# A hybrid streaming layer: the input turned by VectorE in 32x32 blocks, its K tiles made of strided features

## The chip, the core and the metric

One core of one Trainium2 chip runs the whole program. The metric is the device time of one execution in microseconds (us). TensorE (PE) multiplies, with a separate stream of weight loads (PEld); VectorE (DVE), ScalarE (ACT) and GpSimd (POOL) work element by element; SyncE (SP) only starts transfers here. Each engine has its own list of instructions and takes them in the order of that list; engines wait for one another, and for transfers, by semaphores. On-chip data lies in 128 partitions, in SBUF, and TensorE's results in PSUM.

## The reference, cut to what matters

One layer over 256 prompt tokens and 32 sample tokens, 288 columns in all. The change touches the front of it: the input norm and the projection `w_in`.

```
xn   = rmsnorm(x, norm_mix_pre)                 # x: 288 tokens x 2048 features
proj = xn @ w_in                                # 2048 x 5664: [u 1024 | z 2048 | xBC 2560 | dt 32]
pool = pooling mixer on u
ssd  = Mamba-2 scan on xBC and dt, gated by z
x    = x + rmsnorm(concat[pool, ssd] @ w_out, norm_mix_post)
x    = x + rmsnorm(ConvFFN(rmsnorm(x, norm_ffn_pre)), norm_ffn_post)
```

The outputs are the two token blocks and the new states. Everything is float32.

## The kernel before, in words

**Layout.** Activations lie turned: features on partitions, the 288 tokens along the free axis. A product adds one K tile (128 features) into a 128 x 288 accumulator in PSUM. To keep float32 accuracy with a faster product type, every operand is split into a rounded part and a rest: `split_from` (L113) and `split_w` (L134) let ACT write the rounded part (`xn` L120, `whi` L146) and DVE the rest (L121, `wlo` L147), and `mm3` (L162) multiplies three times (L163, L164, L165). The 32 columns of dt are too narrow for that: `split_narrow` (L151) puts both parts side by side in `both` (ACT L158, DVE L159), and two products per K tile do the work (L185, L186).

**The start.** `input_tiles` (L292) loads a slice of x with the tokens on partitions (L294 for the prompt, L295 for the sample), and turns each K tile with three products against the identity (L299, L300, L301) into PSUM. ACT and DVE split it from there, DVE also copies the turned tile to `xT` (L304), and ACT's queue stores `xT` to DRAM in `xT_d` (L306), for the residual much later. The norm's factor per token is not applied here: it multiplies the results of the projection instead.

**The first projection.** `project` (L167) walks over the 16 K tiles in five steps of 2, 2, 4, 4 and 4, with three weight loads in each step: 256 columns of B, 256 of C, 32 of dt (`O_B`, `O_C`, `O_DT`, L338; the load is L131 in `fetch_w`). That is 16 x (4 x 3 + 2) = 224 products into five accumulators (`first`). The squares of x for the norm are summed by ACT (L348, L349), and TensorE spreads the factor `rs` over all partitions with six passes (`prs`, L355). `parameters` (L309) turns the small weights that came as rows, with nine products against the identity (L281, L325).

**What follows** is a long series of projections of 256 columns each: xs (8), z (8) and u (4) from `w_in`, then `w_out`, `w_up` and `w_down`. Weight tiles (`raw`, `whi`, `wlo`) have four buffers each, accumulators five banks, and three more banks (`aux`) serve the rest.

**The order.** The tile framework's scheduler orders each engine's list by priorities. `tc.high_priority` moves an instruction ahead, and `tc.keep_in_program_order`, called `pin` where it has a name, holds instructions of an engine in the order of the program. In the kernel before, the scheduler is free to mix the first projection with the next one, and does so: the last 44 products of the first projection stand after `prs` and among 25 of the first xs projection.

Of the kernel before, what the change touches and what calls it, by code (L numbers as in the profile page):

```python
# [8 lines left out]
F32 = mybir.dt.float32  # L9
F32R = mybir.dt.float32r  # L10
# [6 lines left out]
P = 128  # L17
# [22 lines left out]
XS_RATE = (0, 0, 1, 0, 1, 0, 1, 0)  # L40
Z_RATE = (1, 0, 1, 1, 0, 1, 1, 0)
TAIL = NT - P


@with_exitstack
def body(
# [77 lines left out]
            )  # L124

    ahead = [0]

    def fetch_w(view, kb, nk, c0, nc_):
        raw = wpool.tile([P, nk, nc_], F32, tag="raw", name="raw")
        with tc.high_priority(offset=ahead[0]):  # L130
            sp.dma_start(out=raw, in_=view[:, kb : kb + nk, c0 : c0 + nc_])  # L131
        return raw

    def split_w(raw, kb, nk, nc_, after=()):  # L134

        out = []
        step = min(nk, 1024 // nc_)
        for k in range(0, nk, step):
            n = min(step, nk - k)
            hi = wpool.tile([P, n, nc_], F32R, tag="hi", name="whi")  # L140
            lo = wpool.tile([P, n, nc_], F32R, tag="lo", name="wlo")
            with ExitStack() as order:
                order.enter_context(tc.high_priority(offset=ahead[0]))
                for ins in after:
                    order.enter_context(tc.issue_after(ins.ins))
                act.activation(hi, raw[:, k : k + n, :], AF.Copy)  # L146
                dve.tensor_tensor(lo, raw[:, k : k + n, :], hi.bitcast(F32), op=ALU.subtract)  # L147
            out.append([(kb + k + i, hi[:, i, :], lo[:, i, :]) for i in range(n)])
        return out

    def split_narrow(raw, kb, nk, nc_, after):  # L151

        both = xin.tile([P, nk, 2, nc_], F32R, tag="both", bufs=2, name="both")
        with ExitStack() as order:
            order.enter_context(tc.high_priority(offset=ahead[0]))
            for ins in after:
                order.enter_context(tc.issue_after(ins.ins))
            act.activation(both[:, :, 0, :], raw, AF.Copy)  # L158
            dve.tensor_tensor(both[:, :, 1, :], raw, both[:, :, 0, :].bitcast(F32), op=ALU.subtract)  # L159
        return [(kb + k, both[:, k, :, :].rearrange("p r c -> p (r c)")) for k in range(nk)]  # L160

    def mm3(out, wh, wl, a, start, stop):  # L162
        pe.matmul(out, wh, a[:, 0, :], start=start, stop=False)  # L163
        pe.matmul(out, wh, a[:, 1, :], start=False, stop=False)  # L164
        pe.matmul(out, wl, a[:, 0, :], start=False, stop=stop)  # L165

    def project(view, groups, acts, ksplit, before=None, done=None, spare=(), hold=(), behind=None):  # L167

# [6 lines left out]
        for i, (kb, n) in enumerate(ksplit):  # L175
            raws = [fetch_w(view, kb, n, c0, w) for c0, w in groups]
            nxt = None
            if before and i + 1 < len(ksplit):
                nxt = before(*ksplit[i + 1])
            m0 = 0  # L180
            for raw, (c0, w) in zip(raws, groups):
                if w < P:
                    for k, both in split_narrow(raw, kb, n, w, after or ()):
                        o = accs[m0][: 2 * w, :]
                        pe.matmul(o, both, acts[k][:, 0, :], start=k == k_first, stop=False)  # L185
                        pe.matmul(o, both, acts[k][:, 1, :], start=False, stop=k == k_last)  # L186
                    continue
# [12 lines left out]
            after = nxt  # L200
# [10 lines left out]
    K16 = [(0, 8), (8, 8)]  # L211


    ident = const.tile([P, P], F32, name="ident")
    make_identity(nc, ident)
    ones = const.tile([P, P], F32, name="ones")
    pool.memset(ones, 1.0)
    tri = const.tile([P, P], F32, name="tri")
    pool.affine_select(
        out=tri, in_=ones, pattern=[[1, P]], compare_op=ALU.is_ge, fill=0.0, base=0, channel_multiplier=-1  # L220
# [24 lines left out]
        pool.memset(e, 0.0)  # L245
        ebuf.append(e)

    start = ExitStack()
    xin = start.enter_context(tc.tile_pool(name="xin", bufs=1))

    g0_in = xin.tile([KD, P], F32, name="g0_in")
    act.dma_start(out=g0_in, in_=rows(norm_mix_pre))
# [5 lines left out]
    xt = xin.tile([P, 2, D_MODEL], F32, name="xt")  # L258
    xs_ = xin.tile([NS, D_MODEL], F32, name="xs_")
    xpv = x_prompt.rearrange("o (b p) d -> p (o b) d", p=P)  # L260
# [17 lines left out]
    def columns(src, n, name):  # L278
        o = const.tile([P, n], F32, name=name)
        p_ = aux([P, n], "pt")  # L280
        pe.transpose(p_, src, ident[:n, :n])  # L281
        dve.tensor_copy(o, p_)
        return o

    g_mix_pre = columns(g0_in, KD, "g0")


    xn = []
    xT = xin.tile([P, KD, NT], F32, name="xT")
    xT_d = dram.tile([P, KD, NT], F32, name="xT_d")  # L290

    def input_tiles(kb, n):  # L292
        c = slice(kb * P, (kb + n) * P)
        sp.dma_start(out=xt[:, :, c], in_=xpv[:, :, c])  # L294
        sp.dma_start(out=xs_[:, c], in_=x_sample[0][:, c])  # L295
        for t in range(kb, kb + n):
            p_ = aux([P, NT], "pt")
            c = slice(t * P, (t + 1) * P)
            pe.transpose(p_[:, 0:P], xt[:, 0, c], ident)  # L299
            pe.transpose(p_[:, P:NP_], xt[:, 1, c], ident)  # L300
            pe.transpose(p_[:, NP_:NT], xs_[:, c], ident[:NS, :NS])  # L301
            a = atile("xn")
            last = split_from(a, p_, g_mix_pre[:, t : t + 1])
            dve.tensor_copy(xT[:, t, :], p_)  # L304
            xn.append(a)
        act.dma_start(out=xT_d[:, kb : kb + n, :], in_=xT[:, kb : kb + n, :])  # L306
        return last

    def parameters():  # L309
        pb = columns(pb_in, 108, "pb")  # L310
# [11 lines left out]
        for i in range(0, 6, 3):  # L322
            p_ = aux([P, 3, NF * 2], "ptf")
            for j in range(3):
                pe.transpose(p_[:, j, :], pf_in[:, i + j, :], ident[: NF * 2, : NF * 2])  # L325
            dve.tensor_copy(pf[:, i : i + 3, :], p_)
        return pb, pah, g_mix_post, g_ffn_pre, g_ffn_post, pa, p_scale, g_ssd, pc, pf

    prm = []

    def first_in(kb, n):
        if kb == 12:
            prm.extend(parameters())
        return input_tiles(kb, n)

    win = w_in.rearrange("o (k p) c -> p (o k) c", p=P)
    O_Z, O_X = D_POOL, D_POOL + D_SSD
    O_B, O_C, O_DT = O_X + D_SSD, O_X + D_SSD + 256, O_X + CONV  # L338
    first = project(
        win, [(O_B, 256), (O_C, 256), (O_DT, HEADS)], xn, [(0, 2), (2, 2), (4, 4), (8, 4), (12, 4)], first_in  # L340
    )

    ahead[0] = 200
    ssum = xin.tile([P, 3], F32, name="ssum")
    pool.memset(ssum, 1.0)
    junk = xin.tile([P, D_MODEL], F32, name="junk")
    for b in range(2):
        act.activation(junk, xt[:, b, :], AF.Square, accum_out=ssum[:, b : b + 1])  # L348
    act.activation(junk[:NS, :], xs_, AF.Square, accum_out=ssum[:NS, 2:3])  # L349
    rs = xin.tile([P, 3], F32, name="rs")  # L350
    act.activation(rs, ssum, AF.Sqrt, bias=eps_t, scale=1.0 / D_MODEL)
    dve.reciprocal(rs, rs)
    p_ = aux([P, NT], "prs")
    for b, (o, n) in enumerate(BLK):
        pe.matmul(  # L355
            p_[:, o : o + n], rs[:n, b : b + 1].broadcast_to([n, P]), ident[:n, :n], start=True, stop=True
        )
    rstd = const.tile([P, NT], F32, tag="spread", bufs=3, name="rstd")
    dve.tensor_copy(rstd, p_)

    pb, pah, g_mix_post, g_ffn_pre, g_ffn_post, pa, p_scale, g_ssd, pc, pf = prm
    start.close()
# [509 lines left out]
    for grp in ((0, 1), (2,), (3,), (4,), (5,), (6,), (7,)):  # L872
# [7 lines left out]
        elif grp[0] == 6:  # L880
            late_in[:] = [state_in(t, t >= LATE + 4) for t in range(LATE, NX)]
        if grp[0] == 0:
            sp.dma_start(out=xT, in_=xT_d)
# [148 lines left out]

    p_f = aux([P, 4], "psum_f")
    fd = dram.tile([NT, D_MODEL], F32, name="fd")
    pin = tc.keep_in_program_order

    def to_tokens(t):

# [182 lines left out]
```

## Time and profile before

| | us |
|---|---|
| median of 3 runs (1354.6 to 1355.04) | 1354.8 |
| the profiled execution | 1354.13 |
| its span, from first to last instruction | 1352.2 |
| PE busy in the span | 1340.3 |
| DVE busy | 883.2 |
| ACT busy | 668.8 |
| POOL busy | 237.7 |

A matmul's recorded duration includes the time in which it drains, beside the next one; what a product costs in a dense row is the distance from start to start, 0.13 us for 288 columns. The same holds, more weakly, for DVE and ACT: the next instruction starts some 0.1 us before the recorded end of the one before, unless it waits for it. In the timeline a line gives start, duration, engine, line, operation, output and inputs; in brackets is how long the engine had been idle, and what released it.

### The profile page before, as it was taken

To read this page: it belongs to the slowest core of one execution; us is meant where nothing else is said; L and a number is where in the kernel's file an instruction comes from. 1 tells how busy PE (TensorE), PEld (TensorE's weight loads), DVE (VectorE), ACT (ScalarE), POOL (GpSimd) and SP (SyncE) were. 2 spreads that over 40 slices of the span, in tenths; PEclk is the share of its full clock that TensorE was granted. 3 is DMA by queue.
4 is the path that set the end of the run, shared out by engine and by line. 5 is a ranking of instruction groups with operands and counts; after the bars stand their busy time and mean duration, and the time that the engine had idled before them with its cause. 6 is when DMAs were issued, how large, how long until landed. Compare 5 with 4: busy or idle time off the path is not lost.

```text
span 1352.2 us, 25779 instructions
## 1 busy us (share of the span) xinstructions
PE 1340.3 (99%) x10217; PEld 1328.7 (98%) x10217; DVE 883.2 (65%) x1519; ACT 668.8 (49%) x1004; POOL 237.7 (18%) x394
## 2 busy tenths in 40 slices
PE   8999999999999999999999999999999999999997
PEld 7999999999999999999999999999999999999997
DVE  6898989679644469977666643335666666664444
ACT  5657767446434455644444433334444444454443
POOL 3132112222214310212121100001111111100110
PEclk9999999999999999999999999999999999999999
DMA  8869995465756536866545545554554554576662
GB/s 264 255 192 283 255 263 162 147 219 154 241 181 210 170 111 196 238 174 196 187 156 166 170 145 167 172 179 156 180 164 156 178 166 156 172 231 184 192 182 89
DMA packets 300136, 252.13 MB, mean 186 GB/s; under 512 B 75729, under 2 KB 293051, under 8 KB 299887
## 3 DMA queue, kind: packets, MB, share of 16 engines
q1 hardware_dynamic: 296942, 243.46, 59.4%
q0 software_dynamic: 2320, 4.65, 1.2%
q10 hardware_dynamic: 752, 2.37, 0.5%
q8 instruction: 80, 1.31, 0.4%
q14 instruction: 42, 0.34, 0.1%
HBM read 236.13 MB, written 14.31 MB: 185 GB/s over the span
## 4 chain that ended last, share of the span: by engine, by line
PE 99%; DMA 0%; DVE 0%; ACT 0%; issue 0%; DVEq 0%
PE acc L163 31%; PE acc L165 31%; PE acc L164 31%; PE pst L852 1%; PE py L562 1%; PE acc L1127 1%; PE acc_x L164 0%; PE acc_x L165 0%; PE acc_x L163 0%; PE py L564 0%; DMA xt<-in_x_prompt 0%; PE pt L299 0%; PE pt L301 0%; PE acc L1128 0%; PE acc L186 0%; PE pt L300 0%
## 5 line engine op out<-in xcount | busy, mean ns | idle before, releaser
L147 DVE TENSOR_TENSOR wlo<-raw,whi 128x1024 fp32r<-128x1024 f32 (+1 forms) x416 | 493.2, 1187 | 346.6 <-ACT whi L146 345.5
L146 ACT ACTIVATE whi<-raw 128x1024 fp32r<-128x1024 f32 (+1 forms) x416 | 426.6, 1027 | 483.1 <-PE acc L164 411.0
L163 PE MATMUL acc<-hn,whi 128*128 128x288 f32 x1376 | 404.6, 295 | 0.0
L164 PE MATMUL acc<-hn,whi 128*128 128x288 f32 x1376 | 403.5, 294 | 0.0
L165 PE MATMUL acc<-hn,wlo 128*128 128x288 f32 x1376 | 403.2, 294 | 0.0
L164 PEld LDWEIGHTS acc<-hn,whi 128*128 128x128 f32 x1376 | 259.8, 189 | 0.1
L165 PEld LDWEIGHTS acc<-hn,wlo 128*128 128x128 f32 x1376 | 259.6, 189 | 0.0
L163 PEld LDWEIGHTS acc<-hn,whi 128*128 128x128 f32 x1376 | 257.3, 187 | 0.1
L163 PE MATMUL acc<-xn,whi 128*128 128x288 f32 x704 | 209.3, 299 | 0.0
L164 PE MATMUL acc<-xn,whi 128*128 128x288 f32 x704 | 207.9, 296 | 0.0
L165 PE MATMUL acc<-xn,wlo 128*128 128x288 f32 x704 | 207.0, 296 | 0.0
L163 PE MATMUL acc<-fa,whi 128*128 128x288 f32 x682 | 201.9, 296 | 0.0
L164 PE MATMUL acc<-fa,whi 128*128 128x288 f32 x682 | 201.9, 296 | 0.0
L165 PE MATMUL acc<-fa,wlo 128*128 128x288 f32 x682 | 201.5, 295 | 0.0
L164 PEld LDWEIGHTS acc<-xn,whi 128*128 128x128 f32 x704 | 133.6, 190 | 0.3
L165 PEld LDWEIGHTS acc<-xn,wlo 128*128 128x128 f32 x704 | 132.8, 189 | 0.3
L163 PEld LDWEIGHTS acc<-xn,whi 128*128 128x128 f32 x704 | 132.4, 189 | 0.5
L164 PEld LDWEIGHTS acc<-fa,whi 128*128 128x128 f32 x682 | 128.6, 188 | 0.0
L163 PEld LDWEIGHTS acc<-fa,whi 128*128 128x128 f32 x682 | 128.1, 188 | 0.0
L165 PEld LDWEIGHTS acc<-fa,wlo 128*128 128x128 f32 x682 | 127.9, 188 | 0.0
L944 POOL COPY fc_stage<-ebuf 128x4 f32<-128x4 f32 x88 | 27.2, 309 | 496.6 <-DVE ebuf L943 454.5
L939 POOL COPY ebuf<-pf 128x2 f32<-128x2 f32 x88 | 74.4, 846 | 126.2 <-DVE fc L950 52.4
(337 smaller groups left out, 1680.6 us busy)
## 6 DMA issues: line engine op xcount, KB each, us to landing
raw<-in_w_up SPq DMA_DIRECT2D x80, 1024.0 KB, 5.2
raw<-in_w_in SPq DMA_DIRECT2D x40, 1024.0 KB, 5.8
raw<-in_w_down SPq DMA_DIRECT2D x32, 1024.0 KB, 5.4
raw<-in_w_out SPq DMA_DIRECT2D x24, 1024.0 KB, 6.2
raw<-in_w_down SPq DMA_DIRECT2D x16, 768.0 KB, 4.8
raw<-in_w_up SPq DMA_DIRECT2D x14, 512.0 KB, 4.3
gb<-g_d SPq DMA_DIRECT2D x8, 832.0 KB, 5.7
raw<-in_w_in SPq DMA_DIRECT2D x6, 512.0 KB, 7.1
```

The lines of the kernel that those rows point to most:

```text
L146: act.activation(hi, raw[:, k : k + n, :], AF.Copy)
L147: dve.tensor_tensor(lo, raw[:, k : k + n, :], hi.bitcast(F32), op=ALU.subtract)
L163: pe.matmul(out, wh, a[:, 0, :], start=start, stop=False)
L164: pe.matmul(out, wh, a[:, 1, :], start=False, stop=False)
L165: pe.matmul(out, wl, a[:, 0, :], start=False, stop=stop)
L562: ins = pe.matmul(y[c, 0:256], xw[:, 0, f_], m[:, h, 0:256], start=True, stop=False)
L852: ins = pe.matmul(st[:, o, :], x_, btok[:, gi, b, :], start=b != 1, stop=b != 0)
L939: pool.tensor_copy(e[:, 258:260], pf[:, 4:6, i])
L944: pool.tensor_copy(fc_stage[:, :, :, i], e[:, 256:324].rearrange("p (s c) -> p s c", c=34)[:, :, 0:2])
L1127: pin(pe.matmul(o, hi, f2[k][:, :, c], start=k == 0, stop=end, skip_group_check=True))
```

## The change

- x is loaded as 32-token blocks: partition 32i + t of `xt` holds token t of each of the nine blocks of 32 (eight of the prompt, one of the sample), for features 128i to 128i + 127 of a group of 512. Each of the four groups comes in four transfers of 32 partitions with pieces of 512 bytes.
- A K tile is now every fourth feature of a group of 512: partition p of K tile 4c + j is feature 512c + 4p + j. DVE turns it with one 32x32-block transpose (`input_tile`), reading every fourth element. `norm_mix_pre`, `w_in` and `xT_d` follow that order. Weight loads of `w_in` are cut into groups of four K tiles, so that an 8-tile load is two transfers. The 48 turning products and the copies to `xT` are gone; `xT` is stored by one transfer from SP's queue.
- B, C and dt weights (544 columns) come in one load per step. `FIRST` has nine steps: K tiles 0 and 1 alone, then seven pairs.
- All instructions of this stage are pinned. `prepare(i)` issues, for a pair, on DVE: turn, rest of xn, turn, rest of xn, `wlo`, rest of `both`; on ACT: xn, xn, `whi`, `both`, and from step 4 to 6 three sums of squares.
- `parameters()` stands in step 5. Ahead of step 7's products the steps 7 and 8 are both prepared, then the factor is made: `spots`, one float32 product with `ones` (`prs`), a square root on ACT and a reciprocal of 288 columns on DVE.
- 17 products on a constant tile (`busy`) stand at the head of TensorE's list. g_mix_pre is loaded in columns directly, 16 bytes a piece.

The diff, cut to its core:

```diff
+NB = 512
+FIRST = ((0, 1), (1, 1), (2, 2), (4, 2), (6, 2), (8, 2), (10, 2), (12, 2), (14, 2))
+BUSY = 17
+PARAMETERS = 5
+SQUARES = 4
...
     def fetch_w(view, kb, nk, c0, nc_):
...
+            if len(view.shape) == 4:
+                for c in range(kb // 4, (kb + nk) // 4):
+                    k = 4 * c - kb
+                    sp.dma_start(out=raw[:, k : k + 4, :], in_=view[:, c, :, c0 : c0 + nc_])
...
+    xt = xin.tile([P, 9, 4, P], F32, name="xt")
+    xpv = x_prompt.rearrange("o (b t) (c i w) -> i t (o b) c w", t=NS, i=4, w=P)
+    xsv = x_sample.rearrange("o t (c i w) -> i t (o c) w", i=4, w=P)
+    win = w_in.rearrange("o (c p j) w -> p (o c) j w", p=P, j=4)
...
+    def sample_load(queue, c):
+        for i in range(4):
+            pin(queue.dma_start(out=xt[NS * i : NS * (i + 1), 8, c, :], in_=xsv[i][:, c, :]))
+    def input_load(c):
+        for i in range(4):
+            pin(sp.dma_start(out=xt[NS * i : NS * (i + 1), 0:8, c, :], in_=xpv[i][:, :, c, :]))
+    def first_load(kb, n):
+        raw = wpool.tile([P, n, NB + HEADS], F32, tag="raw", name="raw")
+        pin(sp.dma_start(out=raw, in_=win[:, kb // 4, kb % 4 : kb % 4 + n, O_B : O_B + NB + HEADS]))
+        raws.append(raw)
+    sample_load(act, slice(0, 1))
+    pin(act.dma_start(
+        out=g_mix_pre.rearrange("p (c j) -> p c j", j=4),
+        in_=norm_mix_pre.rearrange("o (c p j) -> p (o c) j", p=P, j=4),
+    ))
+    input_load(0)
+    for kb, n in FIRST[:3]:
+        first_load(kb, n)
+    sample_load(sp, slice(1, 4))
+    input_load(1)
+    first_load(*FIRST[3])
+    input_load(2)
+    input_load(3)
...
-            pe.transpose(p_[:, 0:P], xt[:, 0, c], ident)
-            pe.transpose(p_[:, P:NP_], xt[:, 1, c], ident)
-            pe.transpose(p_[:, NP_:NT], xs_[:, c], ident[:NS, :NS])
...
-            dve.tensor_copy(xT[:, t, :], p_)
...
+    def input_tile(t):
+        pin(dve.transpose(
+            xT[:, t, :].rearrange("p (b t) -> p b t", t=NS),
+            xt[:, :, t // 4, :].rearrange("p b (f j) -> p b f j", j=4)[:, :, :, t % 4],
+        ))
+        a = atile("xn")
+        for ins in split_from(a, xT[:, t, :], g_mix_pre[:, t : t + 1]):
+            pin(ins)
+        xn.append(a)
+    busy_ps = aux([P, NT], "busy_ps")
+    for _ in range(BUSY):
+        pin(pe.matmul(busy_ps, busy[:, 0:P], busy, start=True, stop=True))
...
+    def prepare(i):
+        kb, n = FIRST[i]
+        raw = raws.pop(0)
+        for t in range(kb, kb + n):
+            input_tile(t)
+        (part,) = split_w(raw[:, :, :NB], kb, n, NB, pin=pin)
+        narrow = split_narrow(raw[:, :, NB:], kb, n, HEADS)
+        if i + 4 < len(FIRST):
+            first_load(*FIRST[i + 4])
+        if i >= SQUARES:
+            for b in blocks[:3]:
+                pin(act.activation(junk, xt[:, b].rearrange("p c w -> p (c w)"), AF.Square, accum_out=ssum[:, b : b + 1]))
+            del blocks[:3]
+        if i == PARAMETERS:
+            prm.extend(parameters())
+        return part, narrow
...
+    for i in range(len(FIRST)):
+        if not ready:
+            ready.append(prepare(i))
+        if i + 2 == len(FIRST):
+            ready.append(prepare(i + 1))
+        part, narrow = ready.pop(0)
+        if i + 2 == len(FIRST):
...
+            p_ = aux([P, NT], "prs")
+            pin(pe.matmul(p_, ones, spots.rearrange("p b t -> p (b t)"), start=True, stop=True))
+            rstd = const.tile([P, NT], F32, tag="spread", bufs=3, name="rstd")
+            pin(act.activation(rstd, p_, AF.Sqrt, bias=eps_t, scale=1.0 / D_MODEL))
+            pin(dve.reciprocal(rstd, rstd))
...
```

More of the change, by code (lines that the diff above doesn't have):

```diff
@@ L246, in body @@
         ebuf.append(e)
[L248 to L252, printed above, removed]
     pb_in = xin.tile([108, P], F32, name="pb_in")
@@ L280, in columns @@
         p_ = aux([P, n], "pt")
-        pe.transpose(p_, src, ident[:n, :n])
-        dve.tensor_copy(o, p_)
-        return o
[L285 to L303, printed above, removed]
-            dve.tensor_copy(xT[:, t, :], p_)
-            xn.append(a)
-        act.dma_start(out=xT_d[:, kb : kb + n, :], in_=xT[:, kb : kb + n, :])
-        return last
+        pin(pe.transpose(p_, src, ident[:n, :n]))
+        pin(dve.tensor_copy(o, p_))
+        return o
     def parameters():
@@ L336, in body @@
[L336 to L340, printed above, removed]
-    )
[L343 to L359, printed above, removed]
+    xn = []
@@ new lines, in body @@
+    prm = []
+    ssum = xin.tile([P, 9], F32, name="ssum")
+    junk = xin.tile([P, D_MODEL // 4], F32, name="junk")
+    blocks = list(range(9))
+    first = [acc_ps.tile([P, NT], F32, tag="acc", name="acc") for _ in range(5)]
+    early = ExitStack()
+    early.enter_context(tc.high_priority(offset=2000))
+    def prepare(i):
[12 more added lines that the diff above has]
+        if i == PARAMETERS:
+            prm.extend(parameters())
+        return part, narrow
@@ new lines, in body @@
+    ready = []
+    for i in range(len(FIRST)):
[5 more added lines that the diff above has]
+        if i + 2 == len(FIRST):
+            spots = xin.tile([P, 9, NS], F32, name="spots")
+            sel4 = xin.tile([P, NS], F32, name="sel4")
+            pin(dve.tensor_reduce(sel4, ident.rearrange("p (i t) -> p t i", i=4), axis=AX.X, op=ALU.add))
+            pin(dve.tensor_tensor(
+                spots, ssum.unsqueeze(2).broadcast_to([P, 9, NS]), sel4.unsqueeze(1).broadcast_to([P, 9, NS]), op=ALU.mult
+            ))
+            p_ = aux([P, NT], "prs")
[3 more added lines that the diff above has]
+            pin(dve.reciprocal(rstd, rstd))
+        if not i:
+            (_, hi, lo), = part
+            for w, r in ((hi, 0), (hi, 1), (lo, 0)):
+                for m in range(4):
+                    pin(pe.matmul(first[m], w[:, m * P : (m + 1) * P], xn[0][:, r, :], start=w is hi and not r, stop=False))
+        else:
+            for m in range(4):
+                c = slice(m * P, (m + 1) * P)
+                for k, hi, lo in part:
+                    mm3(first[m], hi[:, c], lo[:, c], xn[k], False, k == KD - 1, pin)
+        for k, both in narrow:
+            o = first[4][: 2 * HEADS, :]
+            pin(pe.matmul(o, both, xn[k][:, 0, :], start=k == 0, stop=False))
+            pin(pe.matmul(o, both, xn[k][:, 1, :], start=False, stop=k == KD - 1))
@@ L361, in body @@
+    early.close()
+    ahead[0] = 200
+    sp.dma_start(
+        out=xT_d.rearrange("(c p j) n -> p c j n", p=P, j=4), in_=xT.rearrange("p (c j) n -> p c j n", j=4)
+    )
     pb, pah, g_mix_post, g_ffn_pre, g_ffn_post, pa, p_scale, g_ssd, pc, pf = prm
```

69 lines of the change are left out of this document (35 added, 34 removed).

## The prediction

> **What bounds the kernel now.** I read the page's busy times first, then what TensorE waited for, then the timeline of the first 52 us, since the change rebuilds that stretch.
>
> ```profile
> PE 1340.3 (99%) x10217; PEld 1328.7 (98%) x10217; DVE 883.2 (65%) x1519; ACT 668.8 (49%) x1004; POOL 237.7 (18%) x394
> ...
> PE 99%; DMA 0%; DVE 0%; ACT 0%; issue 0%; DVEq 0%
> ```
>
> The second line is the chain that ended last: TensorE all the way. Its waits between 11 and 1340 us are one entry:
>
> ```profile
> PE psum_f L1053 <- ACT fsq L1110: 0.2, 1, 0.2
> ```
>
> So from 11.65 us on TensorE is a dense row, and the changed kernel's time is before's plus the shift of the moment at which the first projection's work is done. Nothing later can absorb a shift. TensorE's timeline around three moments:
>
> ```profile
> 10.49 0.44 PE L163 MATMUL acc<-xn,whi 128*128 128x288 f32 x1
> 10.73 0.68 PE L164 MATMUL acc<-xn,whi 128*128 128x288 f32 x2
> ...
> 18.49 0.29 PE L185 MATMUL acc<-xn,both 128*64 128x288 f32 x1
> 18.62 0.27 PE L299 MATMUL pt<-ident,xt 128*128 128x128 f32 x1
> 18.73 0.27 PE L300 MATMUL pt<-ident,xt 128*128 128x128 f32 x1
> 18.93 0.24 PE L301 MATMUL pt<-ident,xs__137 32*128 32x32 f32 x1
> 19.10 0.34 PE L186 MATMUL acc<-xn,both 128*64 128x288 f32 x1
> ...
> 51.30 0.29 PE L186 MATMUL acc<-xn,both 128*64 128x288 f32 x1
> 51.42 0.42 PE L165 MATMUL acc<-xn,wlo 128*128 128x288 f32 x2
> ```
>
> Until 11.65 products start 0.24 us apart, afterwards 0.131. One K tile's turning (18.62 to 19.10, and a late successor) costs TensorE about 0.54 us. The first projection's last product (L186) is over at 51.42, with 25 products of the next one done in between; without these its end would be 51.42 - 25 x 0.131 = **48.1 us**. That is the number to beat.
>
> **The change part by part.** What TensorE loses: 48 turns, 16 x 0.54 = 8.6 us, and six passes of `prs` (0.78 in the chain of waits) become one float32 product of 288 columns (0.49 by `psum_t`, L611). What it keeps: 224 products x 0.131 = 29.3 us. The question is whether DVE and ACT feed them. In the built program's order DVE does per pair: turn a, rest a, turn b, rest b, `wlo`, `both`; ACT: xn a, xn b, `whi`, `both`. Each xn waits for its turn, each rest for its xn, `wlo` for `whi`, and the next turn stands behind `both`. So the steps of a pair stand in one line, whereas before ACT took its input from TensorE and never waited for DVE there. That an instruction that waits holds its whole list is seen in DVE's waits before ("DVE xn L121 <- ACT xn L120: 6.8, 8, 1.8").
>
> Durations, from these rows of DVE's and ACT's timeline:
>
> ```profile
> 31.85 1.21 DVE L147 TENSOR_TENSOR wlo<-raw,whi 128x1024 fp32r<-128x1024 f32 x1
> 32.98 0.28 DVE L159 TENSOR_TENSOR both<-raw,both 128x128 fp32r<-128x128 f32 x1
> 33.18 0.28 DVE L282 COPY pa<-pt 128x124 f32<-128x124 f32 x1
> ...
> 55.57 0.35 DVE L416 TENSOR_SCALAR v<-v,hp 32x288 f32<-32x288 f32 x1
> ...
> 54.56 1.06 ACT L146 ACTIVATE whi<-raw 128x1024 fp32r<-128x1024 f32 x1 [0.37 <-PE acc L164]
> 55.95 0.44 ACT L418 ACTIVATE e__800<-v 32x288 f32<-32x288 f32 x1 [0.34 <-DVE v L416]
> ```
>
> `wlo` to its successor 1.13, `both` to its own 0.20, `whi` 1.06, ACT on 288 columns out of SBUF 0.44, DVE to ACT 0.03 (55.92 to 55.95). The turn is the block transpose of 128x288 (L206), 0.47:
>
> ```profile
> L206 DVE STREAM_TRANSPOSE blocks<-bc x2: 460/470/479, 65.8 to 74.9; 128x288 f32<-128x288 f32 x2
> ```
>
> With 0.04 per hand-over a **pair costs** turn 0.51, xn 0.48, rest 0.43 (L393's spacing in SBUF), turn 0.51, xn to `whi` 0.33, `whi` 1.10, `wlo` 1.13, `both` 0.20: 4.7 us. TensorE needs 28 x 0.131 = 3.67 for it, so it starves by 1.0 us a pair. The turn out of every fourth element has no row. Below: L206's 0.47, which I take, as the nearest in operation and size. Above: 1.93, DVE's slowest operation on 288 columns (reciprocal, L422). It cannot be less than nothing, and a gain on 0.47 is bounded by the 128x256 transpose's 0.38 (L519).
>
> The line from the start:
> - First x group: four transfers on SP's queue and four on ACT's, 0.46 each to issue (L295), so the last goes at 2.2; the first `xt` took 3.2 from issue to TensorE's first turn (0.82 to 4.04): landed at 5.4. The weights of K tile 0 and g_mix_pre wait, in the order built, for one of these eight to be done (about 3.9); a 256 KB weight load took 4.0 (median): 7.9. g_mix_pre took 2.7 (as rows), 16-byte pieces have no row; it has 1 us of room.
> - K tile 0: `whi` 0.67, `wlo` 0.60, `both` 0.20 after 7.9: 9.4. K tile 1: turn 0.51, xn to `whi` 0.33, then the same, that is 2.3: 11.7.
> - Seven pairs, 32.9: 44.6.
> - Squares: three of 512 columns, each about 0.75 by L348's 1.90 for 2048 less 1536 x 0.83 ns (the slope of `whi` from 512 to 1024) and a 0.19 read, make the next xn late by 0.4 in two pairs: 45.4. In the third `parameters` hides them.
> - `parameters`: five copies by DVE with two waits for TensorE, 1.5: 46.9.
> - `spots` stands behind an xs `wlo`: 0.2 + 1.13 + 0.49: 48.7. `prs` waits for it, with the last two pairs' products behind it on TensorE, which has had nothing to do since about 40.4.
> - `prs` 0.5 and 56 products x 0.131 = 7.35: 56.5.
>
> **The clock.** Does TensorE start slowly again after 8 us of idleness? Before has one slow start, from 8.53 or 6.56 to 11.65, 3.1 to 5.1 us at 0.24 instead of 0.131. So the price is between 0 (dense, as after 11.65) and 2.4; by the row, 1.4 to 2.4, I take 1.9: **58.4**. [...]
>
> Sum: 58.4 - 48.1 = +10.3 us. The profiled execution's 1354.13 becomes 1364.4; the median of the runs lies 0.67 above it: **1365.1**.
>
> Costed at nothing, with the cover: the 17 `busy` products (17 x 0.24 = 4.1) lie in TensorE's wait for the first `whi`, until 8.5; DVE's copies for them may be held up as L239's copy was (2.08 beside POOL's memsets), and if they end 1 us late, K tile 1's wait hides that. Two issues per weight load: SP needs 4 x 0.46 per 12.6 us of products. The single `xT` store on SP's queue waits for the last turn (about 43), with xs weight loads behind it that are needed over 20 us later. Square root (table 1.28, 0.45) and the 288-column reciprocal (1.93) run beside the 56 products; the `wlo` behind them on DVE is due 6.3 us after these. The x pieces for step 3 go out as earlier loads are done, the last at about 12 when step 2's weights have landed, and 3.2 later it is 15.2 for a turn due at 16.4: barely covered; a lateness passes to the end in full.
>
> **The rivals.**
> - *TensorE bound, faster.* If the steps of successive pairs overlapped, DVE's own work per pair would count: 2 x 0.43 + 2 x 0.43 + 1.13 + 0.20 = 3.1, below 3.67. Then the end is 8.5 + 29.3 + 0.5 + 0.6 = 38.9, -9.2: 1345.6. It decides below 3.5 us a pair: without the idle time there is no slow clock, the terms other than the pairs are 56.5 - 32.9 = 23.6, and 23.6 + 7 x 3.5 = 48.1. For it speaks only that the busy shares of DVE and ACT leave room; against it the order of the lists.
> - *No slow clock*: 56.5, +8.4: 1363.2.
> - *Turn or loads slower.* At twice 0.47 the 16 turns add 7.5: 1372.6. The 512-byte pieces behind eight transfers in flight may make the first steps 2 to 4 us late: 1367 to 1369.
> - *It cancels*: pairs of 3.1 to 3.9 us without the slow clock, within 2.7 us of before. Nothing speaks for just that.
>
> **How the numbers follow.** Forecast with its slow clock 0.60 (own range: pairs of 4.3 to 5.1 us, start 1 us either way, 1361 to 1369); no slow clock 0.10; slower turn or loads 0.15; TensorE bound 0.10; cancelled 0.05. From 1358 (short pairs, no slow clock, early start) to 1371 (half of the slower turn) is left out: the faster case, the cancelled and some of the slowest, 0.2. A measurement of this kernel tells about 0.2%, 2.7 us, from no change. Slower 0.85, within 0.04, faster 0.11.
>
> **What would show it.** In the changed profile: TensorE waits for `wlo` (DVE) by some 1 us per pair from 11 to 40 us, then 8 us for `spots`; DVE waits for xn and `whi` (ACT) again and again; a turn of about 0.47; 0.24 us between products after `prs`; the first projection's end near 58, and a dense row after it. Wrong if the pairs come every 3.7 us, if the turn isn't near 0.47, or if the row after 58 us has gaps.

## The result, and the profile after

The changed kernel takes 1371.45 us (median of 4 runs, 1370.48 to 1373.88) against 1354.7 for the kernel before: a ratio of 1.0126, 95% interval 1.0114 to 1.0139. It is slower by 16.75 us; 10.3 were forecast. The profiled execution took 1370.48, with a span of 1368.6.

The page of the changed kernel, busy times and the chain that ended last (shares by engine):

```profile
PE 1338.8 (98%) x10181; PEld 1327.1 (97%) x10181; DVE 893.0 (65%) x1525; ACT 670.5 (49%) x1019; POOL 233.7 (17%) x393
...
PE 90%; DMA 5%; DVE 3%; ACT 1%; SPq 1%; issue 1%; DVEq 0%; ACTq 0%
```

Before, the chain was 99% PE. Now it leaves TensorE for transfers (5%) and VectorE (3%). What TensorE waited for between 60 and 1350 us (total, times, longest):

```profile
PE acc L177 <- DVE wlo L159: 1.4, 4, 0.5
PE py L629 <- DVE m L617: 0.8, 2, 0.6
```

Before had two other ones there, both near its end: the 0.2 us that the prediction shows, and at 1344 us

```profile
PE psum_f L1049 <- ACT fsq L1172: 1.1, 1, 1.1
```

So the loss has two places, one in the start and one after it. Two marks separate them. The first is the moment at which the next stage's products begin in a dense row (before, worked out in the same way: 48.1). The second is the first `psum_t` product of the stage after the scan (before: 229.8, that is 181.7 later). On the two timelines, before and then after:

```profile
229.83 0.41 PE L611 MATMUL psum_t<-gsum,ones 128*128 128x288 f32 x1
```

```profile
246.83 0.41 PE L678 MATMUL psum_t<-gsum,ones 128*128 128x288 f32 x1
```

| | next stage begins | `psum_t` begins | from one to the other |
|---|---|---|---|
| before | 48.1 | 229.8 | 181.7 |
| after | 61.7 | 246.8 | 185.1 |

The start lost 13.6 us, the stages from 62 to 247 us another 3.4; that is 17.0 together. From there on the two kernels run nearly alike. The spans end 16.4 apart; the changed kernel doesn't have before's two waits near the end.

**The start.** One pair on VectorE, timeline (start, duration, and in brackets the idle time with its releaser):

```profile
34.13 0.69 DVE L351 STREAM_TRANSPOSE xT<-xt 128x288 f32<-128x288 f32 x1
35.42 0.52 DVE L126 SCALAR_TENSOR_TENSOR xn<-xT,g,xn 128x288 fp32r<-128x288 f32 x1 [0.60 <-ACT xn L125]
35.86 0.69 DVE L351 STREAM_TRANSPOSE xT<-xt 128x288 f32<-128x288 f32 x1
37.16 0.52 DVE L126 SCALAR_TENSOR_TENSOR xn<-xT,g,xn 128x288 fp32r<-128x288 f32 x1 [0.60 <-ACT xn L125]
38.10 1.23 DVE L159 TENSOR_TENSOR wlo<-raw,whi 128x1024 fp32r<-128x1024 f32 x1 [0.43 <-ACT whi L158]
39.24 0.22 DVE L171 TENSOR_TENSOR both<-raw,both 128x64 fp32r<-128x64 f32 x1
39.38 0.70 DVE L351 STREAM_TRANSPOSE xT<-xt 128x288 f32<-128x288 f32 x1
```

and ScalarE in the same pair:

```profile
34.85 0.54 ACT L125 ACTIVATE xn<-xT,g 128x288 fp32r<-128x288 f32 x1 [0.98 <-DVE xT L351]
36.59 0.54 ACT L125 ACTIVATE xn<-xT,g 128x288 fp32r<-128x288 f32 x1 [1.20 <-DVE xT L351]
37.03 1.04 ACT L158 ACTIVATE whi<-raw 128x1024 fp32r<-128x1024 f32 x1
```

Read from start to start, the two engines hand one line of work to and fro: turn 0.72, xn 0.57, rest 0.44, turn 0.73, xn 0.44, `whi` 1.07, `wlo` 1.14, `both` 0.14, in all 5.25 us. TensorE needs 3.67 of them. Neither engine is full: VectorE alone stands 1.6 us per pair for ScalarE.

The end of the first projection on TensorE's timeline:

```profile
51.89 1.33 PE L404 MATMUL prs<-spots,ones 128*128 128x288 f32 x2 [8.81 <-DVE spots L400]
...
53.26 0.44 PE L176 MATMUL acc<-xn,whi 128*128 128x288 f32 x1
53.50 0.44 PE L177 MATMUL acc<-xn,wlo 128*128 128x288 f32 x1
...
55.89 0.30 PE L175 MATMUL acc<-xn,whi 128*128 128x288 f32 x1
56.03 0.29 PE L176 MATMUL acc<-xn,whi 128*128 128x288 f32 x1
...
61.73 0.29 PE L175 MATMUL acc<-xn,whi 128*128 128x288 f32 x1
```

After 8.81 us of idleness the products come 0.24 apart until 55.89, then 0.13 apart; the granted clock was 0.50 from 51.89 to 55.89 and 1.00 from there to 61.7. The last line is the first mark.

**The later loss.** TensorE's six waits after 60 us come at 135.8, 138.5, 142.8, 203.3, 207.1 and 219.5. They add up to 2.3 us of the 3.4; the rest isn't recorded as waiting. VectorE just ahead of the last one, on its timeline:

```profile
217.85 0.48 DVE L212 STREAM_TRANSPOSE blocks<-xs 128x288 f32<-128x288 f32 x1 [4.16 <-DMA xs_d<-blocks]
218.25 1.18 DVE L159 TENSOR_TENSOR wlo<-raw,whi 128x1024 fp32r<-128x1024 f32 x1
```

and TensorE's next wait:

```profile
219.49 0.40 PE L177 MATMUL acc<-xn,wlo 128*128 128x288 f32 x1 [0.46 <-DVE wlo L159]
```

`blocks` is one buffer through which xs goes to DRAM (`blocks_out`, four stores to `xs_d` on SP's queue) to come back as `xk` for the scan. VectorE may not write it again before the stores of the last one have landed. Here it stood 4.16 us for that, and the `wlo` behind it came late for TensorE, by 0.46 us. Of the other waits only the one at 138.5 (0.25) comes right behind a wait of VectorE for `blocks`. The one at 135.8 comes behind a wait for the way back, `xk`. Ahead of those at 203.3 and 207.1 VectorE had last waited for `xk` too, and had worked without a pause since:

```profile
187.66 0.96 DVE L606 TENSOR_TENSOR xw<-xk,tok 128x768 f32<-128x768 f32 x1 [3.48 <-DMA xk<-xs_d]
```

So what is late for TensorE is also a question of what else stands ahead of it on VectorE's list.

### The profile page after: what moved, and what is told of

It is laid out like the page before. It is cut to its first block, busy times and chain, and to the rows that moved or that the text cites. A ratio compares the mean times of both kernels' runs of the same rounds, so it can differ in the third digit from the quotient of the medians.

```text
span 1368.6 us, 25776 instructions
## 1 busy us (share of the span) xinstructions
PE 1338.8 (98%) x10181; PEld 1327.1 (97%) x10181; DVE 893.0 (65%) x1525; ACT 670.5 (49%) x1019; POOL 233.7 (17%) x393
## 4 chain that ended last, share of the span: by engine, by line
PE 90%; DMA 5%; DVE 3%; ACT 1%; SPq 1%; issue 1%; DVEq 0%; ACTq 0%
PE acc L175 29%; PE acc L177 29%; PE acc L176 28%; DMA xs_d<-blocks 2%; DMA raw<-in_w_in 1%; PE pst L919 1%; DVE wlo L159 1%; SPq L215 1%; DMA xt<-in_x_prompt 1%; PE acc L1193 1%; PE py L629 0%; DMA xt<-in_x_sample 0%; ACT whi L158 0%; DVE conv L460 0%; PE acc_x L176 0%
```

## The experiments

The tables and texts give the two marks of one profiled execution, and the median of all runs with the ratio to the kernel before in the same session. Where these disagree, it is said.

Some texts compare the order of the lists. It is read off the traces, as the order of the starts on each engine, from the new stage's first `v` on VectorE to the first `psum_t`. That is 314 to 317 instructions of VectorE.

**The factor's place.** `spots` and `prs` are put ahead of the conversion of the last two K tiles:

```
-        if i + 2 == len(FIRST):
-            ready.append(prepare(i + 1))
         part, narrow = ready.pop(0)
...
             pin(pe.matmul(p_, ones, spots.rearrange("p b t -> p (b t)"), start=True, stop=True))
+            ready.append(prepare(i + 1))
             rstd = const.tile([P, NT], F32, tag="spread", bufs=3, name="rstd")
```

> Only the place of the factor's step changes: spots and the prs product now come ahead of the conversion of the last two K tiles, and square root and reciprocal behind it. Theory (TensorE's 8.8 us of idleness ahead of prs and the slow products behind it are a cost of their own): spots no longer stands behind the last wlo, the products of the pair before run as soon as their own wlo is there, and only the last pair's 28 products come behind the last wlo. First projection's end about 54 us instead of 61.7; time 1371.5 - 7.5 = 1364, with the later loss of 3.3 us unchanged. Rival (the serial line of DVE and ACT alone sets the end, TensorE makes its idleness good): end within 1 us of 61.7, time 1370.5 to 1372.5.

1369.37 us, ratio 1.0106 (1.0092 to 1.012). TensorE's timeline:

```profile
46.21 0.75 PE L402 MATMUL prs<-spots,ones 128*128 128x288 f32 x2 [2.56 <-DVE spots L398]
...
47.65 0.44 PE L175 MATMUL acc<-xn,whi 128*128 128x288 f32 x1
...
50.98 0.30 PE L177 MATMUL acc<-xn,wlo 128*128 128x288 f32 x1
...
58.20 0.37 PE L175 MATMUL acc<-xn,whi 128*128 128x288 f32 x1 [2.29 <-DVE ebuf L447]
```

The wait before `prs` fell from 8.81 to 2.56 us, and the first projection's last product started at 55.63 instead of 61.60: 6.0 us earlier, so the idleness was a cost, and the rival falls. But the gain wasn't kept. The accumulators are emptied with `rstd` (`ebuf`), and the next stage has no free accumulator until 58.20. That took 2.3 us back. `rstd` comes from a square root and a reciprocal that now stand behind the last pair. But it was ready at 53.95, before the first projection's last product; what held `ebuf` longer were three `wlo` of the next stage that stand ahead of it and among it on VectorE's list:

```profile
52.00 1.95 DVE L406 RECIPROCAL rstd<-rstd 128x288 f32<-128x288 f32 x1 [0.60 <-ACT rstd L405]
53.87 2.29 DVE L159 TENSOR_TENSOR wlo<-raw,whi 128x1024 fp32r<-128x1024 f32 x2
56.08 0.75 DVE L446 TENSOR_TENSOR ebuf<-acc,rstd 128x256 f32<-128x256 f32 x2
56.74 1.22 DVE L159 TENSOR_TENSOR wlo<-raw,whi 128x1024 fp32r<-128x1024 f32 x1
57.87 0.28 DVE L447 TENSOR_TENSOR ebuf<-acc,rstd 128x32 f32<-128x32 f32 x2
```

The slow products didn't go either: 0.24 apart from 47.65 to 50.98. And `psum_t` began at 246.9, as in the changed kernel: in this execution, the slowest of its four, the later stages took 188.7 us instead of 185.1. The edit did not leave them alone: 85 of VectorE's 316 instructions there stand in another place than in the changed kernel.

**The turns ahead.** The next step's turns are moved in front of this step's `wlo` on VectorE's list (for step 3 behind `both`, because its x comes later); `turn_step(i)` holds the turns of step i:

```
     def input_tile(t):
-        pin(dve.transpose(
...
     def prepare(i):
...
+        if i == 0:
+            turn_step(0)
         for t in range(kb, kb + n):
             input_tile(t)
+        late = i + 1 == 3
+        if i + 1 < len(FIRST) and not late:
+            turn_step(i + 1)
         (part,) = split_w(raw[:, :, :NB], kb, n, NB, pin=pin)
         narrow = split_narrow(raw[:, :, NB:], kb, n, HEADS)
+        if late:
+            turn_step(i + 1)
```

> Only the order of VectorE's list changes: the turns of the next step are put ahead of this step's wlo, so that they run while ScalarE makes whi. Theory (the steps of a pair stand in one line, DVE to ACT to DVE, and this line is longer than TensorE's 3.67 us of products): a pair costs about 3.7 to 4 us instead of 5.25, spots comes at about 40 instead of 51.4, the first projection ends near 48 instead of 61.7, time about 1357 to 1358 (with the later 3.3 us). Rival (DVE or ACT is busy for those 5 us, or the turns are made slow by what runs beside them): pairs stay above 5 us, the end above 59, time above 1368.

1367.27 us, ratio 1.0094 (1.008 to 1.0108); next stage at 56.8. The line did get shorter: from step 6 to step 7 `wlo` followed `wlo` after 3.9 us (37.15 to 41.08), with 2.2 us of squares on ScalarE in it, and from step 7 to 8, without squares, after 2.1. But only 5 of the 13.7 us came. ScalarE's timeline shows what took the turns' place:

```profile
26.50 1.06 ACT L158 ACTIVATE whi<-raw 128x1024 fp32r<-128x1024 f32 x1 [6.12 <-DMA raw<-in_w_in]
```

The weights of step 4 landed at 26.5, when the line was ready for them at 20.4. In the changed kernel the slow line had hidden that: its `whi` of step 4 starts at 24.89, without a wait for the load.

**The turn's stride.** The same turn out of 32 elements that lie side by side:

```
-  xt[:, :, t // 4, :].rearrange("p b (f j) -> p b f j", j=4)[:, :, :, t % 4],
+  xt[:, :, t // 4, NS * (t % 4) : NS * (t % 4 + 1)],
```

> The turn reads 32 features that lie side by side instead of every fourth; sizes and order are the same. Left out: the right pairing, features meet the weights of other features, so the output is another. Theory A (the step of four elements in the source is what the turn costs above 0.47): turn 0.47 us, a pair 5.25 - 2 x 0.22 = 4.8, the end earlier by at most 16 x 0.22 = 3.5, near 58.2; time about 1368. Theory B (the operation costs 0.69 at this shape whatever its source's step): turn 0.69, end 61.7, time 1371.5.

The turns of the changed kernel and then of this one (ns, smallest, median and largest):

```profile
L351 DVE STREAM_TRANSPOSE xT<-xt x16: 677/688/701, 6.2 to 46.5; 128x288 f32<-128x288 f32 x16
```

```profile
L351 DVE STREAM_TRANSPOSE xT<-xt x16: 468/472/478, 6.1 to 46.5; 128x288 f32<-128x288 f32 x16
```

Theory A holds for the turn: the step of four elements costs 0.22 of 0.69 us. A pair of this kernel takes 4.82 us (`wlo` at 14.61 and 19.43), near the 4.7 of the forecast. The end, though, came at 61.4, not 58.2: the weights of step 4 again, for which ScalarE now stood:

```profile
ACT whi L158 <- DMA raw<-in_w_in: 2.7, 1, 2.7
```

1370.27 us, ratio 1.0114 (1.01 to 1.0128); that is not clearly less than the changed kernel's time. This run and the one before it agree: behind the line of the two engines stood the loads, 25 to 27 us from the start.

**The split loads alone, in the kernel before.**

```
-            sp.dma_start(out=raw, in_=view[:, kb : kb + nk, c0 : c0 + nc_])
+            if nk == 8 and view.shape[-1] == 5664:
+                for k in (0, 4):
+                    sp.dma_start(out=raw[:, k : k + 4, :], in_=view[:, kb + k : kb + k + 4, c0 : c0 + nc_])
+            else:
+                sp.dma_start(out=raw, in_=view[:, kb : kb + nk, c0 : c0 + nc_])
```

> The kernel before, with one part of the change alone: each load of eight K tiles of w_in goes out as two transfers of four K tiles. Theory H1 (the later 3.3 us, gaps of TensorE between 135 and 219 us, come from the doubled transfers, behind which the ones for the scan land later): gaps of some 3 us between 120 and 210 us, time about 1358. Rival H2 (they come from the changed order in which the scheduler sets out the work of these stages, or from something else in the start): no such gaps, time 1354.7 within 0.7.

1354.74 us, ratio 1.0001 (0.9992 to 1.001). TensorE had one wait of 0.8 us between 60 and 230 us. H1 falls: in the old order of the lists the doubled transfers don't make the later loss.

**Two `blocks` buffers in the changed kernel.**

```
-        s = pool_.tile([P, NT], F32, tag="blocks", bufs=1, name="blocks")
+        s = pool_.tile([P, NT], F32, tag="blocks", bufs=2 if pool_ is mp else 1, name="blocks")
```

> The changed kernel with two blocks buffers in the mixer's stages instead of one; nothing else is edited. Theory (the later 3.3 us: VectorE stands before blocks until the stores of the last one have landed behind weight loads on SP's queue, and what is behind it, wlo and m, comes late for TensorE): VectorE's waits on xs_d<-blocks between 60 and 222 us go from 10.8 us to under 3, TensorE's gaps between 130 and 222 us from 3.3 to under 1, time about 1368.5. Rival (it is the order of the work of these stages that makes wlo and m late; the store's wait is only where VectorE happens to stand): gaps of 2.5 to 4 us remain, time 1370.5 to 1372.5.

1369.12 us, ratio 1.0102 (1.0089 to 1.0115). VectorE's waits on these transfers between 60 and 230 us, first with one buffer, then with two:

```profile
DVE blocks L212 <- DMA xs_d<-blocks: 10.8, 7, 4.2
DVE xw L606 <- DMA xk<-xs_d: 6.5, 4, 3.5
```

```profile
DVE xw L606 <- DMA xk<-xs_d: 4.8, 4, 1.8
...
DVE blocks L212 <- DMA xs_d<-blocks: 1.1, 1, 1.1
```

TensorE had no wait between 63.5 and 222 us, and the marks are 181.4 apart: the later loss is gone. What took it away is not settled by this run. The edit is one line, but the scheduler answered it with another order: 70 of VectorE's 317 instructions of these stages stand elsewhere than in the changed kernel, while the lists of the start are the same. So the rival, the order, isn't excluded. In this execution the next stage began only at 63.3: ScalarE waited 1.0 us for the weights of step 4, and the slow products behind `prs` lasted until 58.31. Neither has to do with the edit, and both hide a part of its gain in this profile.

**Turns ahead, and the loads in another order.** The third and fourth group of x go out after the weights of steps 4 and 5 instead of before them:

```
-    input_load(2)
-    input_load(3)
...
             first_load(*FIRST[i + 4])
+        if i < 2:
+            input_load(2 + i)
```

> The turns ahead of wlo as in the run before, and the third and fourth group of x behind the fifth and sixth weight load on SP's queue instead of ahead of them. Theory (with the turns ahead, the weights of step 4, landed at 26.5, were the next bound): whi of step 4 starts near 23 instead of 26.5, the first projection ends at 53 to 53.5 instead of 56.8, time about 1363.5. Rival (the first 25 us are bound by what all loads together take, whatever their order): the end stays above 56, time 1366.5 to 1368.

1366.74 us, ratio 1.009 (1.0077 to 1.0103); next stage at 55.1, and `psum_t` at 244.6. The wait for step 4's weights went, and a moment later ScalarE stood for 7.8 us before the first sum of squares, which needs the last group of x. (The profile puts it down to a weight load; the squares read x alone.) The theory named the right wait but not what was late next. The profiled execution was the slowest of four, and the median doesn't differ from that of the turns alone.

**The same with the factor early.**

> The same, and spots and prs ahead of the conversion of the last two K tiles. Theory (TensorE's idle time before prs, 4.3 us with the turns ahead, is lost): the pair's products before the last run while the last is converted, end 3 us earlier than without it (about 50), less a wait of up to 2.3 us for ebuf, since rstd comes later; time 1361 to 1363. Rival (the wait for ebuf takes it all): end of the first projection earlier, first product of the next stage no earlier, time as without it (1363.5).

1364.12 us (1359.6 to 1366.86), ratio 1.0064 (1.005 to 1.0077), above the theory's 1361 to 1363. The profiled execution was the slowest of the six. The next stage began at 50.7, as the theory said, 11 us earlier than in the changed kernel. But `psum_t` began at 243.3, only 3.5 earlier. The later stages took 192.6 us. TensorE's timeline there:

```profile
129.40 0.65 PE L638 MATMUL py<-m,xw 128*64 128x256 f32 x4 [2.07 <-DVE m L626]
```

```profile
201.91 0.61 PE L177 MATMUL acc<-xn,wlo 128*128 128x288 f32 x1 [4.70 <-DVE wlo L159]
```

Ahead of that second gap VectorE stood not for `blocks` but for `xk`; then it made `xw`, `m` and, without a wait, `blocks`, and only then the `wlo`:

```profile
197.17 0.96 DVE L615 TENSOR_TENSOR xw<-xk,tok 128x768 f32<-128x768 f32 x1 [3.02 <-DMA xk<-xs_d]
```

**No busy products** (`BUSY = 1` for 17).

> The changed kernel with one busy product instead of 17. Theory (the 17 do nothing for the end: TensorE was idle for 2.7 us behind them, K tile 0's products ran slow all the same, and K tile 1 was waited for): end of the first projection 61.7, time 1371.5 within 0.7. [...]

1371.93 us, ratio 1.0126 (1.0113 to 1.0139); next stage at 61.95 against 61.73, K tile 0's products slow for 3.5 us against 3.3. The 17 products do nothing for the end.

**All of it: turns, loads, factor, two buffers.**

> Turns ahead, loads reordered, factor early, and two blocks buffers: the run with the first three had the first projection's end at 50.7 and gaps of TensorE of 7.5 us between 125 and 205. Theory (the gaps come from VectorE's wait for the one blocks buffer, whatever moment the stages start at): no gaps after 52 us, time 1364.1 - 7.5 = 1356.6, within 1.5. Rival (the gaps come with an early start of these stages, since transfers lag behind TensorE): gaps of 2 to 7 us stay, time 1359 to 1364.

1358.46 us, ratio 1.0027 (1.0016 to 1.0039), a little above the range of the theory's number. The next stage began at 53.5 in this execution (9.6 us of slow products in its start), `psum_t` at 235.2: 181.7 apart, no loss. The rival falls: an early start alone doesn't bring the gaps. Again the second buffer came with another order: 63 of VectorE's 317 instructions stand elsewhere than in the run with three edits.

**The squares one step later** (`SQUARES = 5` for 4), on top of that.

> The same with the squares one step later (steps 5 to 7 instead of 4 to 6). With the loads reordered, ScalarE's first square stood 6.7 us for the last group of x, with the next pair behind it, and TensorE 4.8 us for that. Theory (that wait is on the path): it goes, the first projection ends 2.5 to 4 us earlier, at 46.5 to 48, time 1353 to 1354.5, at or a little below the kernel before. Rival (the weights of step 5, or the squares' 2.2 us in the next three pairs, take its place): the end stays at 50 to 51, time as without the edit.

1355.45 us, ratio 1.0007 (0.9998 to 1.0016): the kernel before's time again. The first projection's end, 48.1, is at the late edge of the theory's range, and the time lies 0.95 us above its range. TensorE's timeline at the end of the start, where only the wait for `ebuf` is left of what the first experiment had turned up:

```profile
49.02 0.37 PE L175 MATMUL acc<-xn,whi 128*128 128x288 f32 x1 [0.79 <-DVE ebuf L457]
```

**One buffer again, in that kernel.**

> The run with all edits, back to one blocks buffer. The start is then as early as there (next stage's first product at 49.0), and only the later stages differ. Theory (with one buffer these stages have a bound of their own: in the runs with one buffer psum_t began at 243 to 248, whether the next stage began at 50.7 or at 62; an early start is given back): psum_t at 241 to 245 instead of 230.8, gaps of TensorE of 6 to 10 us between 110 and 222, time 1364 to 1368. Rival (each edit's gain stands by itself, and one buffer costs the 3.4 us that it cost in the changed kernel): psum_t at 234, time about 1359.

1360.11 us (1359.31 to 1363.27), ratio 1.004 (1.0026 to 1.0054). The profiled execution was the longest of the five: marks at 49.5 and 239.8, 190.3 apart. In the medians the second buffer, with the order that comes with it, is worth 4.7 us at this early start and 2.3 in the changed kernel. The truth lies between the two theories: a part of an early start is lost again with one buffer, but not most of it.

**Two buffers in the kernel before.**

> The kernel before with two blocks buffers in the mixer's stages. Theory (before has the same waits of VectorE on stores, 10 us in 60 to 230, but its TensorE had no gap to lose): 1354.7 within 0.7. Rival (the waits cost something there too): below 1354.

1357.77 us, ratio 1.0016 (1.0007 to 1.0025): slower, which neither side had. VectorE's waits on the way through DRAM between 60 and 230 us, in before itself (TensorE had none there):

```profile
DVE blocks L206 <- DMA xs_d<-blocks: 10.0, 4, 3.5
DVE xw L539 <- DMA xk<-xs_d: 1.3, 1, 1.3
```

and VectorE's and TensorE's with two buffers:

```profile
DVE xw L539 <- DMA xk<-xs_d: 11.0, 3, 4.6
PE acc L165 <- DVE wlo L147: 2.1, 1, 2.1
```

The waits on `blocks` are gone there too, and in their place VectorE stands for `xk`, the way back from DRAM. The new buffer let the scheduler set out these stages in another order (53 of VectorE's 315 instructions stand elsewhere), and in this one TensorE waits 2.1 us. So one buffer or two isn't the whole cause. In both cases VectorE stands for the detour over DRAM, and the likely reading is that the order decides what is behind it on the list.

The marks side by side, with the number of `blocks` buffers and the order of VectorE's list in the later stages. Runs with the same letter have the same list there, or one with at most five instructions elsewhere:

| run | buffers | order | next stage begins | `psum_t` begins | apart | median |
|---|---|---|---|---|---|---|
| before | 1 | A | 48.1 | 229.8 | 181.7 | 1354.7 |
| before, two buffers | 2 | B | 49.3 | 233.6 | 184.3 | 1357.77 |
| after | 1 | C | 61.7 | 246.8 | 185.1 | 1371.45 |
| no busy products | 1 | C | 62.0 | 248.3 | 186.3 | 1371.93 |
| contiguous turn | 1 | C | 61.4 | 246.2 | 184.8 | 1370.27 |
| turns ahead | 1 | C | 56.8 | 243.0 | 186.2 | 1367.27 |
| turns, loads | 1 | C | 55.1 | 244.6 | 189.5 | 1366.74 |
| factor early | 1 | D | 58.2 | 246.9 | 188.7 | 1369.37 |
| turns, loads, factor | 1 | D | 50.7 | 243.3 | 192.6 | 1364.12 |
| the same, squares later | 1 | D | 49.5 | 239.8 | 190.3 | 1360.11 |
| two buffers alone | 2 | E | 63.3 | 244.7 | 181.4 | 1369.12 |
| four edits | 2 | F | 53.5 | 235.2 | 181.7 | 1358.46 |
| four edits, squares later | 2 | F | 49.0 | 230.8 | 181.8 | 1355.45 |

The five runs of order C have the same lists on VectorE, ScalarE, GpSimd and the SP queue, without one exception, while their start moved by 7 us: the loss stayed. In order D it stayed with a start at 49.5, close to before's 48.1. So a late start isn't what makes it. With one buffer the rebuilt kernel loses 3 to 11 us in each of eight runs, with two nothing in each of three. In four of the eight (factor early; turns, loads; turns, loads, factor; squares later) the profiled execution was the slowest, 1.0 to 3.2 us above its median, so the larger figures are partly chance. No order of these was run with both numbers of buffers, so the two can't be told apart. None of the versions beats the kernel before.

## Why the prediction was right and wrong

Right in sign and in the mechanism of the start: the steps of a pair stand in one line, and the line is longer than TensorE's work. Wrong in the size of the pair, and in the step that carried the start's shift unchanged to the end. The start came 3.3 us later than forecast and the stages behind it lost 3.4 more; without either of the two the time would still have lain within the range from 1358 to 1371. Of what the prediction named as signs of being wrong, two came: the turn was not near 0.47, and the row after the start had gaps. Its terms against the changed kernel's profile:

| step | forecast | measured |
|---|---|---|
| K tile 1 converted | 11.7 | 11.4 |
| seven pairs | 7 x 4.7 = 32.9 | 7 x 5.25 = 36.8 |
| squares | 0.8 | 0.3 |
| `parameters` | 1.5 | 1.5 |
| to the end of `spots` | 1.8 | 1.9 |
| `prs` and 56 products, 1.9 of it slow clock | 9.7 | 9.9 |
| next stage | 58.4 | 61.7 |

- **The mis-sized term is the pair**, 0.56 us each, 3.9 in all. "Turn 0.51" was 0.72: of the two bounds, 0.47 and 1.93, the lower was taken, as the nearest in operation and size, though that row (`blocks<-bc`) reads elements side by side and the turn every fourth. The contiguous turn shows that this is the cause, 0.472 against 0.688; why the step costs 0.22 us, no run shows. "xn 0.48" was 0.57 and "xn to `whi`" 0.33 was 0.44: the row used for ScalarE out of SBUF had 32 partitions and no per-partition factor, and which of these makes 0.54 out of 0.44 was not tried. The measured pair of 5.25 us lies outside the prediction's own 4.3 to 5.1.
- **"Nothing later can absorb a shift" was the step that failed.** It was drawn from before's dense row, and it was taken to mean that nothing later can be lost either. The rebuilt start came with another order of the stages behind it (117 of VectorE's 315 instructions stand elsewhere than in before), and in that order what VectorE makes came late for TensorE: 3.4 us. Before had waits on `blocks` as well, 10.0 us, and none of them reached TensorE. The dense row shows what one order did, not what any order will do.
- **The slow clock** was right: 1.9 taken, 2.0 measured (9.9 us for what takes 0.5 + 7.35 with products 0.131 apart), at a granted clock of 0.50 for the first 4.0 us of it.
- **The eight microseconds for `spots`** were right (8.81). That they cost something was only half right: with most of them gone the end was 6.0 us earlier, but 2.3 went to `ebuf` and the slow products stayed.
- **The rivals.** The measured time lies where "turn or loads slower" had its 1367 to 1372.6: the turn was slower by half, and the loads were the next bound behind it, hidden at 26 us. That rival alone would have given 1365.1 + 3.5 = 1368.6 for 0.22 a turn. "TensorE bound" was far: even with the turns ahead the loads held step 4.
- **Costs put at nothing**: the 17 busy products (1371.93 with one of them) and the two issues per load (1354.74 in the kernel before) did cost nothing. x for step 3 came in time, as said, barely: the run with the turns ahead, which wanted it earlier, got it at 16.2, and the changed kernel's turn started at 16.65.

What stays open is which part of the change makes the scheduler set out the later stages in an order that loses time, and whether the second buffer helps by itself or by the order that comes with it. The split of the loads was tried in before's order and makes no such loss there. The moment at which these stages start is excluded by the table: the order stayed while the start moved, and so did the loss. That the order decides is argued, from before's loss with two buffers and from the gaps that stand behind waits for `xk`.

## What to carry to other kernels

Give an operation that reads with a step the price of a row that reads with that step, or keep the upper bound: the nearest row by size was off by half (0.47 taken, 0.69 measured). When a wait is taken out, write down what is late next: here it was the turns, then the weights of step 4, then the last x for the squares, then `ebuf`, and only all of them together brought the time back. And a dense row of TensorE is no proof that the stages in it have slack: look at the waits of the engines that feed it, and at the buffers they wait for, before calling a shift constant. Where a scheduler sets the order, compare the lists before and after an edit: a second buffer looked like an edit of one thing, and moved 70 instructions.

## What the runs showed of the hardware

The slow products don't need 8 us of idleness. TensorE's timeline of the run with the factor early, in the start:

```profile
12.88 0.30 PE L420 MATMUL acc<-xn,both 128*64 128x288 f32 x1
15.24 0.40 PE L175 MATMUL acc<-xn,whi 128*128 128x288 f32 x1 [2.07 <-ACT whi L158]
...
16.50 0.40 PE L177 MATMUL acc<-xn,wlo 128*128 128x288 f32 x1 [0.73 <-DVE wlo L159]
16.74 0.40 PE L175 MATMUL acc<-xn,whi 128*128 128x288 f32 x1
16.93 0.45 PE L176 MATMUL acc<-xn,whi 128*128 128x288 f32 x1
...
20.05 0.36 PE L177 MATMUL acc<-xn,wlo 128*128 128x288 f32 x1
20.26 0.30 PE L175 MATMUL acc<-xn,whi 128*128 128x288 f32 x1
```

Waits of 2.07 and 0.73 us were followed by 3.3 us of products 0.24 apart, which began when TensorE was already at work again. In the run with the four edits waits of 1.45 and 1.37 us (to 18.79 and to 20.68) were followed by 5.75 us of them. The changed kernel's profile has waits of 1.75 and 0.73 us in the same place (to 15.39 and to 16.65) with no slow products behind them; its K tile 0 was slow from 8.19 to 11.47, at a granted clock of 0.50, and the four edits' start had 9.6 us of slow products where the same code with later squares had 6.2, in another place. So waits of 1 to 2 us cost a slow stretch in some executions and none in others, and their length alone doesn't decide it. Behind the 17 busy products K tile 0 ran slow in the changed kernel, after a wait of 2.68 us, and dense in the run with the factor early, after 1.94 us (its first 12 products from 8.05 to 9.75). What sets off these slow stretches, and what ends them after 3.3 us in one execution and 5.75 in another, no run shows.
